# Expert products in plain float32 on two column halves, and expert weights stored in load order

## The chip, the cores and the metric

The kernel runs on one core of a Trainium2 chip. The metric is the device time of one execution, in microseconds (us), as the median of several runs. The engines are named as in the profile: PE is TensorE's matrix multiply, PEld its weight load, DVE is VectorE, ACT is ScalarE, POOL is GpSimd, and SP is the engine whose queue starts nearly all loads.

## What is computed

512 tokens of width 1024 pass through two blocks. The first has two layers, each with a gated recurrence, three kinds of attention and a feed-forward part. The second has two attentions, a cross attention to a memory, and at its end a mixture of 32 experts. The change touches the experts alone. The reference for one expert and its tokens is

```python
def expert_block(args):
    xb, e = args
    hb = jax.nn.silu(xb @ w_gate[e]) * (xb @ w_up[e])
    return hb @ w_down[e]
```

Every token goes to two experts of one group, and the two results are added with weights `row_w` to the residual; a last norm follows. `w_gate` and `w_up` are 1024 x 512 per expert and `w_down` is 512 x 1024, all float32, so that one expert has 3 x 2 MB (6.29 MB) of weights and all 32 have 201 MB. All of it is read in each run, since each expert gets tokens.

## The kernel before

The scheduler of the language sets the order of the instructions on each engine; buffers come from pools whose sizes stand in `CAPS` (SBUF) and `PSUM_BUFS` (PSUM). A tile is written again only when all that read it are done, and this is how loads are held back: a load on SP waits until its buffer is free.

The experts stand in `moe`. Routing makes lists of up to 64 places (`CAP`) per expert. Then a loop over the 32 experts runs. `gather` (L1485, an indirect DMA that POOL issues) brings the expert's token rows from `x_d` into one of two buffers `xg`. `front` transposes them on PE (L1493, eight transposes into the PSUM tile `PU`), multiplies by the norm's gain on DVE into `ex`, and runs the gate and the up product. `back` transposes the 64 x 512 hidden rows (L1520, four transposes), runs the down product, copies the result out on ACT (L1532) and scatters the rows to `y_d` with another indirect DMA from POOL (L1533). `back` of an expert comes after `front` of the next.

Every product is made of numbers split in two: `split` writes the high part of a tile in the type float32r on ACT (L258) and the remainder on DVE (L259), and `mm3` (L282 to L284) adds three products, high by high, low of the one by high of the other and the reverse. The token side is stationary, 128 x 64 (64 token places), and the weights are the moving side, 512 columns a matmul. Per expert these are 8 row blocks x 2 products x 3 plus 4 row blocks x 2 halves x 3, or 72 matmuls.

`weights` (L1475) takes a buffer `ew` of 128 x 1024 (512 KB), loads it and splits it into `ewh` and `ewl`. There are 34 buffers `ew`. A tile of the gate or up weights is two row blocks of 128 x 512, so that each partition receives two runs of 2 KB; a tile of the down weights is one row block of 128 x 1024, one run of 4 KB per partition, and 512 KB in one piece in memory. The first 34 loads are started early, in groups, each gated on an event further ahead in the program (`gate`, a copy of one column on POOL): ten, then up to 16, 24 and 32, and the last two when the lists are there.

After the loop come, in the program's text, the loads of the residual by tokens (`xt`, L1557), a diagonal matrix of the tokens' weights built by eight POOL instructions (`dg`, L1560), an identity (`idn`, L1563), a conditional block for experts with more than 64 tokens (L1576, not taken here), and the sum of both experts of each token on PE (L1597, L1606) with the last norm. All engines meet at the end of the conditional block.

Of the kernel before, what the change touches and what calls it, by code (L numbers as in the profile page):

```python
# [20 lines left out]
            hh=22, hl=22, gt=10, sq=2, fw=2, fwh=2, fwl=2, yh=8, yl=8, mgh=8, mgl=8, MKH=4, MKL=4, yt=4, xt=4, ew=34, ew1=16, ew2=24, ew3=32, xgs=2, ewh=3, ewl=3, exh=2, exl=2, esg=2, ex=2, ehh=2, ehl=2, ey=3, fs=4, fo=4)  # L21
# steps of a layer of the first block, see Net.layer1
# [9 lines left out]
# ---------------------------------------------------------------- host layout  # L32
# Constants that depend on shapes alone, and inputs rearranged (no arithmetic).
# [5 lines left out]
def _constants():  # L39
# [56 lines left out]
    # what the last phase needs comes first  # L96
# [10 lines left out]
def _masks():  # L107
    """[128, 3, 128]: causal mask, strictly earlier rows, identity; and the forget rows' selectors"""
    p = np.arange(128)
    m = np.zeros((128, 10, 128), np.float32)  # L110
    m[:, 0] = np.where(p[None, :] > p[:, None], NEG, 0.0)
    m[:, 1] = p[:, None] < p[None, :]
    for h in range(8):
        m[h, 2 + h] = 1.0
        m[32 + h, 2 + h] = 1.0
    return m
# [41 lines left out]
def _chunks(w, starts, size=128):  # L158
    """[K, N] -> per chunk [128, K/128 * size]: the blocks of a column chunk, K blocks in order."""
# [4 lines left out]
def _flat(w, width=1024):  # L164
    """[n, 128, W] -> tiles of `width` columns of the row of blocks."""
    a = w.transpose(1, 0, 2).reshape(128, -1)
    return np.ascontiguousarray(a.reshape(128, -1, width).transpose(1, 0, 2))


def _layout(inp):  # L170
# [46 lines left out]
    o["eg"] = x["w_exp_gate_2"][0]  # L217
    o["eu"] = x["w_exp_up_2"][0]
    o["ed"] = x["w_exp_down_2"][0]
# [7 lines left out]
# ---------------------------------------------------------------- the kernel  # L227


class Net:  # L230
# [3 lines left out]
    # ---- small helpers  # L234
# [4 lines left out]
    def column(self, n):  # L239
        """a few columns of their own, for the whole program"""  # L240
# [3 lines left out]
    def after(self, t, gate):  # L244
        """t's first write comes after `gate` is there."""
# [8 lines left out]
    def split(self, hi, lo, src, scale=None):  # L254
        """hi + lo = src (* scale per partition), both float32r."""
# [8 lines left out]
    def wload(self, ap, width, lane=""):  # L264
        """weights in two parts; lane f: buffers of their own, for products that fill other phases' gaps"""
# [12 lines left out]
    def mm3(self, ps, wst, wmv, first, last):  # L278
        """ps += (h + l of stationary)(h + l of moving), three passes."""
# [30 lines left out]
    def wstream(self, ap, lane=""):  # L310
        """blocks [128, 128] of tiles ap[n][128, 1024] in order."""
# [7 lines left out]
    def chunk(self, stream, xs, n=512, out=None):  # L319
        """one column chunk of 128 outputs: W^T x, x a list of (hi, lo)."""  # L320
# [5 lines left out]
    # ---- norm: x * gain in two parts, and 1/rms apart  # L326
# [26 lines left out]
    def sums(self, ps, sq, ones, nb, w=1, rows=slice(0, 128)):  # L353
        """column sums of sq [.., nb * 128] by token: ps[:, (b w)] = sq_b^T ones"""
# [3 lines left out]
    def rows(self, r):  # L358
        """columns r[t, i] as rows [i, t] of a scratch in memory"""
# [11 lines left out]
    def spread_pe(self, ps, r, nb, rows=128, stride=1, at=0):  # L371
        """ps[:rows, (b t)] = r[t, b], the same in every partition"""
# [6 lines left out]
    def spread(self, out, d, nb, at=0, stride=1):  # L379
        """out[p, (b t)] = row b of d, the same in every partition"""  # L380
# [4 lines left out]
    def rsqrt(self, out, ms, scale, eps):  # L385
        """out = (ms * scale + eps) ** -0.5 on a few columns: first guess from the bits, three Newton steps."""
# [16 lines left out]
    def tokens(self, ap, ntile, kper, n, xs, rtok, nb, evac, lane=""):  # L403
        """token-major projection: out[b] [128 tokens, n], W [128, kper, n] tiles."""
# [12 lines left out]
    def half_silu(self, out, ps, rstd):  # L417
        """out = silu(ps * rstd) as (tanh(z / 2) + 1) * z / 2"""
# [19 lines left out]
    def head_sums(self, ps):  # L438
        """mean squares of raw heads by token: sums [128, (4 blocks, 2 heads)]"""
# [6 lines left out]
    def nsa_q(self, ps, gain, cos, sin, rtok):  # L446
        """raw roped q times gain as two stacks; per token and head rstd / 8."""
# [8 lines left out]
    def head_rsqrt(self, r, ms, rtok, scale, eps):  # L456
        """rtok * (rtok^2 * ms * scale + eps) ** -0.5 for [128, (4 blocks, 2 heads)]"""
# [30 lines left out]
    def q_stack(self, x, n=512):  # L488
        """heads of rows 0-63 and 64-127 -> two [hi; lo] stacks."""
# [10 lines left out]
    def k_stack(self, x, n=512, into=None):  # L500
        """per head [hi; hi] and [lo; lo]."""
# [16 lines left out]
    # ---- softmax rows  # L518
# [16 lines left out]
    def softmax_rows(self, Ps, scores, scale=None, gate=None):  # L535
        """of the four query blocks: exp(scale * (S - max)) * gate / row sum"""
# [20 lines left out]
    def softmax(self, P, S, n, scale=None):  # L557
        """exp(scale * (S - max)), its row sum's reciprocal."""
# [11 lines left out]
    def transposed(self, Ps, causal=True, two=True):  # L570
        """P of the four query blocks -> per key block ((hi, lo) or the whole, first query column)."""
# [28 lines left out]
    def values(self, n, name, two):  # L600
        """two: per head of 64 its two parts side by side"""
# [11 lines left out]
    def pv(self, out, v, p, first, last):  # L613
        """two parts: rows 0-63 high part of v times p, rows 64-127 low part of v times the high part of p"""
# [12 lines left out]
    def out_heads(self, O, row0, hi, lo):  # L627
        """O psum [64, 512] -> rows row0.. of the chunk's hi / lo."""
# [10 lines left out]
    # ---- block 1  # L639
# [37 lines left out]
    def compress(self, l, n):  # L677
        """the compressed keys [hi; hi], [lo; lo] of [128, (g 32)], and values per head."""
# [3 lines left out]
        for i, s in enumerate("kv"):  # L682
# [10 lines left out]
            # the 32nd block does not exist: its column is never used  # L693
# [73 lines left out]
    def cmp_probs(self, l, n, g):  # L767
# [4 lines left out]
        for qb in range(4):  # L772
# [18 lines left out]
            if qb == 0:  # L791
                # queries before the first whole block see none
# [6 lines left out]
    def nsa_head(self, l, n, h, hi, lo):  # L799
        """one query head: the three branches, gated, summed in one bank."""  # L800
# [16 lines left out]
    def hgrn_proj(self, l, xs, rstd):  # L817
        """log forget gates, keys and queries of the two pairs of heads."""
# [27 lines left out]
    def hgrn_levels(self, l, r):  # L846
        """A[s, t] = sum_d q_t k_s exp(b_t - b_s), s <= t, built over halved spans, two heads at a time.
# [850 lines left out]
```

## Time and profile before

| what | value |
| --- | --- |
| three runs | 2646.52, 2654.74, 2651.53 us; median 2651.53 us |
| span of the profiled execution | 2651.4 us |
| PE busy | 2582.3 us, 97% |
| DVE busy | 1816.4 us, 69% |
| ACT busy | 1334.6 us, 50% |
| POOL busy | 134.4 us, 5% |
| bytes read from memory | 370.61 MB, of which 201 MB are expert weights |

The profiled execution's own time is its span; it lies 0.1 us under the median of the runs. A PE row's busy time runs from a matmul's start to its modelled end, and successive matmuls overlap, so that the time one costs in a row of equal ones is the distance from start to start, not the duration. A plain float32 matmul of 512 columns leaves two records in the trace (for example, the eight of L1300 leave 16).

### The profile page before, as it was taken

How to read it: one execution, taken by the hardware profiler on the slowest of the kernel's cores; microseconds unless marked ns; L12 is line 12 of the kernel's file. 1: busy time of each engine (PE TensorE's matmuls, PEld its weight loads, DVE VectorE, ACT ScalarE, POOL GpSimd, SP SyncE). 2: the span in 40 equal slices, each digit the busy share in tenths (PEclk: the TensorE clock that was granted, in tenths of full speed). 3: DMA queues.
4: the chain of work that ended last, by engine and by line, in shares of the span. 5: the costliest groups of instructions: out<-in, count | busy, mean ns of one | idle time of the engine just before them, and what ended most of it. 6: DMA issues, size and time to landing. Idle time of an engine off the chain costs nothing. (4 is left out here: it accounts for less than half of the span.)

```text
span 2651.4 us, 33625 instructions
## 1 busy us (share of the span) xinstructions
PE 2582.3 (97%) x12098; PEld 1862.6 (70%) x12099; DVE 1816.4 (69%) x3496; ACT 1334.6 (50%) x2026; POOL 134.4 (5%) x199
## 2 busy tenths in 40 slices
PE   8999999999999999999999999999997999999997
PEld 6876557888888875678888877777874555555553
DVE  6778875444346888864443378677665989888986
ACT  6544553222235445442222256554443777877784
POOL 0000000000000000000000000000011110111102
PEclk9999999999999999999999999999997999999998
DMA  5132002222231231012222231222246999999996
GB/s 199 42 106 78 9 17 90 93 95 96 96 126 58 65 118 34 1 64 95 93 92 96 95 115 56 84 92 83 92 175 237 329 342 344 338 348 350 338 344 244
DMA packets 144316, 382.32 MB, mean 144 GB/s; under 512 B 15744, under 2 KB 16144, under 8 KB 143504
## 3 DMA queue, kind: packets, MB, share of 16 engines
q1 hardware_dynamic: 138160, 369.62, 41.0%
q0 software_dynamic: 5120, 8.40, 1.0%
q10 hardware_dynamic: 864, 2.10, 0.3%
q8 instruction: 96, 1.57, 0.2%
q14 instruction: 76, 0.62, 0.1%
HBM read 370.61 MB, written 12.59 MB: 145 GB/s over the span
## 5 line engine op out<-in xcount | busy, mean ns | idle before, releaser
L258 ACT ACTIVATE wh<-w 128x1024 fp32r<-128x1024 f32 (+1 forms) x264 | 276.5, 1048 | 642.8 <-PE mm L283 352.0
L282 PE MATMUL mm<-xh,wh 128*128 128x512 f32 x1232 | 494.7, 402 | 9.9 <-ACT wh L258 9.9
L283 PE MATMUL mm<-xl,wh 128*128 128x512 f32 x1232 | 493.7, 401 | 0.0
L284 PE MATMUL mm<-xh,wl 128*128 128x512 f32 x1232 | 491.3, 399 | 0.7 <-DVE wl L259 0.7
L259 DVE TENSOR_TENSOR ewl<-ew,ewh 128x1024 fp32r<-128x1024 f32 x384 | 450.8, 1221 | 50.5 <-ACT ewh L258 48.1
L259 DVE TENSOR_TENSOR wl<-w,wh 128x1024 fp32r<-128x1024 f32 (+1 forms) x264 | 319.6, 1211 | 172.8 <-ACT wh L258 171.6
L258 ACT ACTIVATE ewh<-ew 128x1024 fp32r<-128x1024 f32 x384 | 377.8, 1047 | 14.3 <-PE mm L284 5.1
L282 PEld LDWEIGHTS mm<-xh,wh 128*128 128x128 f32 x1232 | 232.8, 189 | 66.6 <-ACT wh L258 10.0
L283 PEld LDWEIGHTS mm<-xl,wh 128*128 128x128 f32 x1232 | 232.6, 189 | 55.5 <-issue 2.9
L284 PEld LDWEIGHTS mm<-xh,wl 128*128 128x128 f32 x1232 | 232.7, 189 | 54.0 <-DVE wl L259 1.5
L252 DVE TENSOR_TENSOR tmp<-mm,xrstd 128x512 f32<-128x512 f32 x104 | 71.6, 690 | 250.6 <-PE mm L284 244.1
L283 PE MATMUL mm<-hl,wh 128*128 128x512 f32 x352 | 138.6, 394 | 0.0
L282 PE MATMUL mm<-hh,wh 128*128 128x512 f32 x352 | 138.3, 393 | 0.0
L284 PE MATMUL mm<-hh,wl 128*128 128x512 f32 x352 | 138.2, 393 | 0.0
L549 ACT ACTIVATE P<-S,st,const 128x128 f32<-128x128 f32 (+3 forms) x128 | 78.5, 616 | 52.7 <-DVE st L252 43.0
L282 PE MATMUL mm<-ewh,exh 128*64 128x512 f32 x256 | 102.0, 398 | 1.8 <-ACT exh L258 1.8
L282 PE MATMUL S<-ewh,ehh 128*64 128x512 f32 x256 | 102.4, 400 | 1.0 <-ACT ehh L258 1.0
L283 PE MATMUL mm<-ewl,exh 128*64 128x512 f32 x256 | 102.5, 400 | 0.0
L284 PE MATMUL mm<-ewh,exl 128*64 128x512 f32 x256 | 101.8, 398 | 0.4 <-DVE exl L259 0.4
L283 PE MATMUL fmm<-ewl,exh 128*64 128x512 f32 x256 | 101.6, 397 | 0.0
L282 PE MATMUL fmm<-ewh,exh 128*64 128x512 f32 x256 | 100.6, 393 | 0.5 <-ACT ewh L258 0.5
L284 PE MATMUL fmm<-ewh,exl 128*64 128x512 f32 x256 | 100.6, 393 | 0.0
(514 smaller groups left out, 4779.7 us busy)
## 6 DMA issues: line engine op xcount, KB each, us to landing
ew<-in_eg_dram SPq DMA_DIRECT2D x128, 512.0 KB
ew<-in_eu_dram SPq DMA_DIRECT2D x128, 512.0 KB
ew<-in_ed_dram SPq DMA_DIRECT2D x128, 512.0 KB
w<-in_fi_dram SPq DMA_DIRECT2D x88, 512.0 KB
w<-in_w_dram SPq DMA_DIRECT2D x48, 512.0 KB
w<-in_fo_dram SPq DMA_DIRECT2D x44, 512.0 KB
w<-in_c_dram SPq DMA_DIRECT2D x16, 512.0 KB
tmp<-tmp SPq DMA_DIRECT2D x80, 64.0 KB
```

What stands on the lines that cost most here:

```text
L252: (eng or self.nc.vector).tensor_tensor(out, a, b, op=op)
L258: nc.scalar.activation(hi, src, AF.Copy)
L259: nc.vector.tensor_tensor(lo, src, hi.bitcast(F32), op=OP.subtract)
L282: nc.tensor.matmul(ps, ah, bh, start=first, stop=False)
L283: nc.tensor.matmul(ps, ah, bl, start=False, stop=False)
L284: nc.tensor.matmul(ps, al, bh, start=False, stop=last)
L549: nc.scalar.activation(Ps[q0 + i], S[:, :n], AF.Exp, bias=b, scale=1.0 if scale is None else scale[q0 + i], accum_out=st[:, 1, i:i + 1])
```

## The change

The expert matmuls use plain float32 tiles: nothing is split, and one `matmul` stands where `mm3` stood. The gate product writes PSUM partitions 0 to 63 and the up product partitions 64 to 127 of one PSUM tile, that is, the 64 stationary columns of the one lie in the left half of the array and those of the other in the right half, and the two take turns. The down product does the same with its two halves of 512 columns. Each expert now has 24 such matmuls. The factor 1/rms of a token is applied to the gathered rows on ACT (L1487) and no longer behind the product. The hidden rows are copied out of PSUM once (L1513). The gate and up loads alternate on SP.

The host lays the three weight arrays out as [expert, 4, 128, 1024], so that each load of 512 KB is one piece in memory with one run of 4 KB per partition. There are 40 buffers `ew`, and 8 of them (before: 2) wait for the lists. Comments and docstrings are gone too; lines that held them are empty or removed, and this moves no instruction.

```diff
-            hh=22, ..., ew=34, ew1=16, ew2=24, ew3=32, xgs=2, ewh=3, ewl=3, exh=2, exl=2, esg=2, ex=2, ehh=2, ehl=2, ey=3, fs=4, fo=4)
+            hh=22, ..., ew=40, ew1=16, ew2=24, ew3=32, xgs=2, esg=2, eh=2, ex=2, ehT=2, ey=3, fs=4, fo=4)
...
-    o["eg"] = x["w_exp_gate_2"][0]
-    o["eu"] = x["w_exp_up_2"][0]
-    o["ed"] = x["w_exp_down_2"][0]
+    for n, w in (("eg", "gate"), ("eu", "up"), ("ed", "down")):
+        e = x[f"w_exp_{w}_2"][0]
+        o[n] = np.ascontiguousarray(e.reshape(NE, -1, 128, e.shape[2]).transpose(0, 2, 1, 3).reshape(NE, 128, 4, 1024).transpose(0, 2, 1, 3))
...
         def weights(ap):
             w = self.tile([128, 1024], F32, name="ew")
...
-            nc.sync.dma_start(w.rearrange("p (a b) -> p a b", b=ap.shape[-1]), ap)
-            wh = self.tile([128, 1024], F32R, name="ewh")
-            wl = self.tile([128, 1024], F32R, name="ewl")
-            if self.nw <= CAPS["ewh"]:
-                self.gate(wh, rt)
-                self.gate(wl, ready)
-            self.split(wh, wl, w)
-            return wh, wl
+            nc.sync.dma_start(w, ap)
+            return w
...
+        one, two_ = slice(0, CAP), slice(CAP, 2 * CAP)
+
         def front(xg, li_e, wg, wu, pool="mm"):
+            nc.scalar.activation(xg[:CAP], xg[:CAP], AF.Copy, scale=li_e[2])
             pt = self.mmT(self.ptn)
...
-            self.split(xh.rearrange(f3), xl.rearrange(f3), x.rearrange(f3))
-            pss = []
-            for w3 in (wg, wu):
-                ps = self.mmT(pool)[:CAP]
-                for t in range(4):
-                    wh, wl = weights(w3[:, 2 * t:2 * t + 2, :])
-                    for kk in range(2):
-                        k = 2 * t + kk
-                        ws = slice(kk * 512, kk * 512 + 512)
-                        self.mm3(ps, (xh[:, k, :], xl[:, k, :]), (wh[:, ws], wl[:, ws]), k == 0, k == 7)
-                pss.append(ps)
-            sg = self.tile([CAP, 512], F32, name="esg")
-            nc.scalar.activation(sg, pss[0], AF.Silu, scale=li_e[2])
-            nc.vector.scalar_tensor_tensor(sg, pss[1], li_e[2], sg, op0=OP.mult, op1=OP.mult)
-            return sg
+            ps = self.mmT(pool)
+            for t in range(4):
+                ws = [weights(w3[t]) for w3 in (wg, wu)]
+                for kk in range(2):
+                    k = 2 * t + kk
+                    for r, w in zip((one, two_), ws):
+                        nc.tensor.matmul(ps[r], x[:, k, :], w[:, kk * 512:kk * 512 + 512], start=k == 0, stop=k == 7)
+            sg = self.tile([128, 512], F32, name="esg")
+            nc.scalar.activation(sg[two_], ps[one], AF.Silu)
+            h = self.tile([CAP, 512], F32, name="eh")
+            self.tt(h, ps[two_], sg[two_], OP.mult)
+            return h
...
-            py = [self.mmT("S")[:CAP] for _ in range(2)]
+            hT = self.tile([128, 4, CAP], F32, name="ehT")
+            nc.vector.tensor_copy(hT.rearrange(f3), pt[:, :256])
+            py = self.mmT("S")
             for k in range(4):
-                wh, wl = weights(wd[:, k:k + 1, :])
-                for half in range(2):
-                    ws = slice(half * 512, half * 512 + 512)
-                    self.mm3(py[half], (hh[:, k, :], hl[:, k, :]), (wh[:, ws], wl[:, ws]), k == 0, k == 3)
+                w = weights(wd[k])
+                for i, r in enumerate((one, two_)):
+                    nc.tensor.matmul(py[r], hT[:, k, :], w[:, i * 512:i * 512 + 512], start=k == 0, stop=k == 3)
```

The order on PE around the border of two experts in the middle of the loop, before. `mm` and `S` are PSUM tiles of the gate and of the down product, `PU` takes transposes, `exh` and `ehh` are the high parts of the tokens and of the hidden rows:

```order
L282 MATMUL mm<-ewh,exh 64x512
L283 MATMUL mm<-ewl,exh 64x512
L284 MATMUL mm<-ewh,exl 64x512
L1520 MATMUL PU<-const,esg 128x64 x3
L1493 MATMUL PU<-const,xg_15883 128x64 x8
L282 MATMUL S<-ewh,ehh 64x512
L283 MATMUL S<-ewl,ehh 64x512
```

The same engine and place now. `mm` and `fmm` hold gate and up side by side, `eh` are the hidden rows:

```order
L1499 MATMUL mm<-ew,ex 64x512 x16
L1518 MATMUL S<-ew,ehT 64x512 x2
L1511 MATMUL PU<-const,eh 128x64 x4
L1490 MATMUL PU<-const,xg_15881 128x64 x7
L1518 MATMUL S<-ew,ehT 64x512 x2
L1490 MATMUL PU<-const,xg_15881 128x64
L1518 MATMUL S<-ew,ehT 64x512 x4
L1499 MATMUL fmm<-ew,ex 64x512 x16
```

The triples became single matmuls that read the loaded tile `ew` itself, and the last pair of a down product moved behind the next expert's sixteen gate and up matmuls.

The order on POOL at the end of the loop, before (the last scatters, then what the end of the kernel needs; `TENSOR_LOAD` reads the number that the conditional block tests):

```order
L1533 DMA y_d<-ey,const 1024x1024 x3
L1560 TENSOR_SCALAR ew<-const 128x128 x8
L1533 DMA y_d<-ey,const 1024x1024
L1575 TENSOR_LOAD cmaxi
L249 COPY idn<-ey 64x1
L1563 COPY idn<-const 128x128
L1533 DMA y_d<-ey,const 1024x1024
L1576 COMPARE_AND_BRANCH
```

And now:

```order
L1522 DMA y_d<-ey,const 1024x1024 x5
L249 COPY idn<-ey 64x1
L1552 COPY idn<-const 128x128
L1522 DMA y_d<-ey,const 1024x1024
L1549 TENSOR_SCALAR ew<-const 128x128 x8
L1564 TENSOR_LOAD cmaxi
L1565 COMPARE_AND_BRANCH
```

The eight instructions for the diagonal matrix `dg`, which stood ahead of the last two scatters, now stand behind the last one and ahead of the branch.

## Rows read from the trace of the kernel before

**Rows 1.** Page, the span in 40 equal slices, two of its rows:

```profile
DMA  5132002222231231012222231222246999999996
GB/s 199 42 106 78 9 17 90 93 95 96 96 126 58 65 118 34 1 64 95 93 92 96 95 115 56 84 92 83 92 175 237 329 342 344 338 348 350 338 344 244
```

**Rows 2.** Windows: stretch, its us, then PE, PEld, DVE, ACT, POOL, clock, DMA, GB/s:

```profile
2060.00:2600.00 540.00, 538.52 (x2513) 311.40 (x2512) 485.18 (x480) 427.86 (x510) 57.90 (x60) 1.00 0.98 343
```

**Rows 3.** Groups of PE in 2060 to 2600, by form: busy us, mean ns:

```profile
L282 PE MATMUL S<-ewh,ehh 128*64 128x512 f32 x240 | 96.0, 400 | 0.0
...
L1493 PE MATMUL PU<-const,xg 64*128 64x64 f32 x239 | 19.8, 223 | 0.0
L1520 PE MATMUL PU<-const,esg 64*128 64x64 f32 x117 | 19.4, 246 | 0.0
```

**Rows 4.** Line L1533, 2060 to 2600: count, ns min/median/max, first and last start:

```profile
L1533 POOL DMA_INDIRECT y_d<-ey,const x30: 897/924/1524, 2073.1 to 2596.1; - x30
```

**Rows 5.** Waits of SP in 2060 to 2600: waited for, us, times, longest:

```profile
SPq L1475 <- DVE ewl L259: 359.4, 274, 5.1
```

**Rows 6.** The gathers' and scatters' DMA queue in 2060 to 2600: packets, MB, share of 16 engines:

```profile
q0 software_dynamic: 4560, 7.65, 4.5%
```

**Rows 7.** Three float32 matmuls of 36 stationary columns: timeline, then their line:

```profile
1996.04 2.77 PE L1300 MATMUL tok<-h,const 128*36 128x512 f32 x6
...
L1300 PE MATMUL tok<-h,const x16: 592/592/620, 1996.0 to 2013.7; 128*36 128x512 f32 x16
```

**Rows 8.** Timeline of L377, 64 stationary columns: two halves in turn, then one alone:

```profile
215.73 1.76 PE L377 MATMUL X<-tmp,const 128*64 128x512 f32 x4
...
216.42 0.19 PEld L377 LDWEIGHTS X<-tmp,const 128*64 128x64 f32 x2 [0.52 <-DVE tmp L376]
...
274.02 1.07 PE L377 MATMUL X<-tmp,const 128*64 128x512 f32 x2
```

**Rows 9.** Windows as in Rows 2, where many loads stand in the queue:

```profile
1956.00:1974.00 18.00, 13.31 (x62) 10.74 (x60) 11.71 (x27) 5.37 (x11) 5.11 (x19) 0.88 1.04 387
1994.00:1997.00 3.00, 3.00 (x12) 1.57 (x12) 2.18 (x4) 1.08 (x2) 0.00 (x0) 1.00 1.02 418
2027.00:2031.00 4.00, 1.99 (x24) 1.91 (x20) 2.31 (x8) 0.00 (x0) 0.55 (x2) 0.50 1.03 420
```

**Rows 10.** Timeline of SP: start, us, the loads that filled these stretches, and the later ones:

```profile
1955.57 9.32 SPq L1475 DMA_DIRECT2D ew<-in_eg_dram  x4
...
1990.34 1.76 SPq L1475 DMA_DIRECT2D ew<-in_ed_dram  x4
...
2035.71 3.66 SPq L1475 DMA_DIRECT2D ew<-in_eg_dram  x3
```

**Rows 11.** Timeline of PE where the experts begin:

```profile
2038.66 0.66 PE L282 MATMUL mm<-ewh,exh 128*64 128x512 f32 x1 [0.69 <-ACT exh L258]
```

**Rows 12.** Timelines of PE, POOL and SP at the end of the kernel:

```profile
2619.37 0.40 PE L284 MATMUL S<-ewh,ehl 128*64 128x512 f32 x1
...
2620.97 0.92 POOL L1533 DMA_INDIRECT y_d<-ey,const  x1 [0.49 <-ACTq L1576]
...
2626.14 1.99 SPq L1604 DMA_DIRECT2D yt<-y_d  x4
```

**Rows 13.** Line L1560, all eight, then the three from 2606.8 on:

```profile
L1560 POOL TENSOR_SCALAR ew<-const x8: 592/1838/2535, 2597.0 to 2608.0; 128x128 f32<-128x128 f32 x8
...
L1560 POOL TENSOR_SCALAR ew<-const x3: 592/595/1324, 2605.5 to 2607.4; 128x128 f32<-128x128 f32 x3
```

**Rows 14.** Windows as in Rows 2, with PE partly idle:

```profile
1010.50:1017.40 6.90, 5.05 (x24) 2.68 (x22) 6.78 (x33) 4.23 (x12) 0.00 (x0) 1.00 0.00 0
829.60:833.00 3.40, 2.17 (x17) 1.70 (x15) 2.12 (x3) 2.77 (x3) 0.00 (x0) 1.00 0.41 126
833.10:839.80 6.70, 6.70 (x27) 6.12 (x27) 4.41 (x8) 2.59 (x4) 0.00 (x0) 0.50 0.02 6
2017.50:2044.70 27.20, 12.11 (x76) 8.76 (x77) 17.17 (x51) 6.03 (x9) 9.25 (x28) 0.50 0.77 269
```

More of the change, by code (lines that the diff above doesn't have):

```diff
@@ L20 @@
             P=2, P2=2, pth=3, ptl=3, st=8, stc=2, r4=2, rsx=3, rsy=3, rst=3, hr=2, xtok=2, mh=8, ml=8,
-            hh=22, hl=22, gt=10, sq=2, fw=2, fwh=2, fwl=2, yh=8, yl=8, mgh=8, mgl=8, MKH=4, MKL=4, yt=4, xt=4, ew=34, ew1=16, ew2=24, ew3=32, xgs=2, ewh=3, ewl=3, exh=2, exl=2, esg=2, ex=2, ehh=2, ehl=2, ey=3, fs=4, fo=4)
+            hh=22, hl=22, gt=10, sq=2, fw=2, fwh=2, fwl=2, yh=8, yl=8, mgh=8, mgl=8, MKH=4, MKL=4, yt=4, xt=4, ew=40, ew1=16, ew2=24, ew3=32, xgs=2, esg=2, eh=2, ex=2, ehT=2, ey=3, fs=4, fo=4)
 ORDER = "P0 L0 A0 V0 O0 O1 W0 K0 Q0 Q1 C0 H0 H1 H2 H3 K1 Q2 Q3 C1 H4 H5 H6 H7 R0 R1"
@@ L1493, in front, with back @@
                 nc.tensor.transpose(pt[:, k * 64:k * 64 + 64], xg[:CAP, k * 128:k * 128 + 128], self.c("ident")[:CAP, :CAP])
[L1494 to L1496 removed]
             x = self.tile([128, 8, CAP], F32, name="ex")
             self.tt(x, pt.rearrange("p (k n) -> p k n", k=8), self.p("g_ffn")[:, :, None].to_broadcast([128, 8, CAP]), OP.mult)
[L1499 to L1515 removed]
+            ps = self.mmT(pool)
[10 more added lines that the diff above has]
+            return h
+        def back(h, li_e, wd):
             f3 = "p a b -> p (a b)"
@@ L1519, in back @@
             for k in range(4):
-                nc.tensor.transpose(pt[:, k * 64:k * 64 + 64], sg[:, k * 128:k * 128 + 128], self.c("ident")[:CAP, :CAP])
-            hh = self.tile([128, 4, CAP], F32R, name="ehh")
-            hl = self.tile([128, 4, CAP], F32R, name="ehl")
-            self.split(hh.rearrange(f3), hl.rearrange(f3), pt[:, :256])
-            py = [self.mmT("S")[:CAP] for _ in range(2)]
+                nc.tensor.transpose(pt[:, k * 64:k * 64 + 64], h[:, k * 128:k * 128 + 128], self.c("ident")[:CAP, :CAP])
+            hT = self.tile([128, 4, CAP], F32, name="ehT")
+            nc.vector.tensor_copy(hT.rearrange(f3), pt[:, :256])
+            py = self.mmT("S")
             for k in range(4):
-                wh, wl = weights(wd[:, k:k + 1, :])
-                for half in range(2):
-                    ws = slice(half * 512, half * 512 + 512)
-                    self.mm3(py[half], (hh[:, k, :], hl[:, k, :]), (wh[:, ws], wl[:, ws]), k == 0, k == 3)
+                w = weights(wd[k])
+                for i, r in enumerate((one, two_)):
+                    nc.tensor.matmul(py[r], hT[:, k, :], w[:, i * 512:i * 512 + 512], start=k == 0, stop=k == 3)
             y = self.tile([CAP, D], F32, name="ey")
-            for half in range(2):
-                nc.scalar.activation(y[:, half * 512:half * 512 + 512], py[half], AF.Copy)
+            for i, r in enumerate((one, two_)):
+                nc.scalar.activation(y[:, i * 512:i * 512 + 512], py[r], AF.Copy)
             nc.gpsimd.indirect_dma_start(
@@ L1538, in wviews @@
         def wviews(e):
-            return [self.a[n][e].rearrange("(k p) f -> p k f", p=128) for n in ("eg", "eu", "ed")]
+            return [self.a[n][e] for n in ("eg", "eu", "ed")]
         lists = [[li[:CAP, 0, e:e + 1], li[:CAP, 1, e:e + 1], rtp[:CAP, e:e + 1]] for e in range(NE)]
@@ L1587, in moe @@
                         gather(xgs[0], lists)
-                        w = [v.rearrange("a k p f -> p (a k) f") for v in
-                             [self.a[n][bass.ds(e, 1)].rearrange("a (k p) f -> a k p f", p=128) for n in ("eg", "eu", "ed")]]
+                        w = [self.a[n][bass.ds(e, 1)].rearrange("a k p f -> (a k) p f") for n in ("eg", "eu", "ed")]
                         back(front(xgs[0], lists, w[0], w[1]), lists, w[2])
```

4 lines of the change are left out of this document (removed).

## The prediction

> **What bounds the kernel now.** I read the page's 40 slices first. In the last nine the DMA engines are busy nine tenths or more, at some 340 GB/s [rows 1]; that is the stage of the experts, and two suspects show: PE and the loads. The windows then say that from 2060 to 2600 us PE is busy 538.5 of 540 us at a granted clock of 1.00 (2.4 GHz), with a DMA share of 0.98 [rows 2]. A DMA share does not tell who waits for whom. SP's waits do: for 359.4 us it stood before the next load because the remainder split `ewl` on DVE had not yet released a buffer [rows 5]. So the loads are held back by their readers, the readers keep pace with PE, and PE never waits: **PE bounds the stage**. Its pace is read from the scatters, one per expert: (2596.1 − 2073.1)/29 = 18.03 us [rows 4]. The transposes of an expert take (19.8 + 19.4)/30 = 1.3 us [rows 3], which leaves 16.7 us for 72 matmuls, 0.232 us each.
>
> **PE's work per expert.** 72 split matmuls become 24 plain ones of 512 columns. The price of a plain one is in the trace of another stage: six records of L1300 take 2.77 us, the last one 0.592, so records start (2.77 − 0.592)/5 = 0.436 us apart, and two of them make a matmul of 0.87 us [rows 7]. If the two column halves exclude each other, an expert costs 24 × 0.87 + 1.3 = 22.2 us; if they run fully at once, 12 × 0.87 + 1.3 = 11.8 us. Which it is hangs on one place of the trace. L377 runs two plain float32 matmuls of 64 stationary columns on two halves. The second half's weights waited for DVE and were in at 216.42 + 0.19; the pair ended at 215.73 + 1.76 = 217.49, 1.07 us after 216.42. A lone one of the same line takes 1.07 us as well [rows 8]. Had the second half waited for the first, whose last record cannot have ended before about 216.2 + 0.59 = 216.8, it would have ended near 217.9. So the halves overlapped, though for some 0.4 us of a single pair only. I take 0.9 to 0.95 us for a pair and 12.1 to 12.7 us for an expert; both ends, 11.8 and 22.2, stay for the rivals. The pair at which nothing is gained is (18.03 − 1.3)/12 = 1.39 us.
>
> **The loads become the bound.** With PE at about 12.5 us, an expert's twelve loads decide. Before, they ran at 343 GB/s at a share of 0.98, or 350 if always busy: 512 KB in 1.50 us. That was with two thirds of the bytes in runs of 2 KB. Where many loads stand in the queue, the 2 KB runs of `eg` moved at 387 GB/s, the 4 KB runs of `ed` at 418 and 420, with PE busy or half idle [rows 9]; [rows 10] has the loads that filled the first two stretches. In the changed kernel all three arrays have the form of `ed`, and the queue is deep, since PE is quicker than the loads. At 418 GB/s a load takes 1.25 us. These rows last only 3 to 4 us, so I take 2% off and use 1.28 us; 1.25 and 1.50 us bound the range. The gathers and scatters take 4.5% of the engines, 0.045 × 540/30 = 0.81 us per expert [rows 6]. Period: 12 × 1.28 + 0.81 = 16.2 us. So of PE's gain of about 5.5 us per expert some 3.7 us are lost to the loads.
>
> The Trainium skill, "DMA: Bandwidth & Descriptors" (Bandwidth), speaks against more than about 358 GB/s from memory when both cores of a pair stream, and lets a lone core go higher; the rows with 418 and 420 agree with the lone core. By the lower figure, as an estimate, a load would take 1.46 us and the kernel about 2612 us.
>
> **Start and end of the stage.** Groups of early loads are gated as before: 32 of 384 loads are started ahead, and the next begin on SP at 2035.7 [rows 10], so 352 loads run from about 2036.5: 352 × 1.28 = 450.6 us. The gathers and scatters of 29.3 experts add 23.8. The last load lands at 2036.5 + 450.6 + 23.8 = 2510.9. PE's first expert matmul stays at about 2038.7 [rows 11], with 32 to 40 tiles in hand, and at 1.05 us per tile against 1.28 it catches up after some 150 tiles; from there it follows each load. Its cold start, clock 0.50 until 2044.7 [rows 14], is therefore hidden; without that lead it would cost some 5 us. After the last load one pair is left, 0.9 us: 2511.8.
>
> Before, the kernel ended 2651.4 − 2619.8 = 31.6 us after its last expert matmul (2619.37 + 0.40 [rows 12]). This tail stays with one addition. The eight instructions for `dg` on POOL ran before the last scatters; now they stand between the last scatter and the branch at which all engines meet, and the loads of `yt` stand behind that on SP. One takes 0.592 us when DVE is quiet, up to 2.5 when it is not [rows 13]: 8 × 0.592 = 4.7 us. The scatter's issue ended at 2621.9 and `yt` began at 2626.1 [rows 12], so POOL or the scatter's landing already took 4.2 us there. If `dg` runs beside the landing it costs about 0.5, if the landing comes first, all 4.7; I take 4. The loads of `xt` now queue behind the last expert's, 2.6 MB at 418 GB/s or 6.3 us; the branch and `yt` come later than that, which hides them. Uncovered they would cost up to 6.3.
>
> Sum: 2511.8 + 31.6 + 4 = **2547 us**, against the profiled execution's own 2651.4 (the median of the runs is 2651.53; I correct nothing for 0.1 us). The bounds: 1.25 us per load and no delay by `dg` give 2533; 1.50 us give 2036.5 + 528 + 23.8 + 36.5 = 2624.
>
> **Costed at nothing:** DVE's and ACT's splits (DVE 485 us and ACT 428 us busy of 540 [rows 2], most of it splits) stood beside PE, and nobody waits for them afterwards. The new scaling of the gathered rows on ACT is some 1 us between gather and transposes; the gather for an expert is started when the buffer of the one before is free, a period of 16 us ahead, and covers it. If the gather came late it would be 1 us per expert, 30 us in all. The 40 instead of 34 `ew` buffers add lead, not rate.
>
> **Rivals.** *Halves exclude each other (slower).* Against it stands the pair of rows 8, for it that this is one pair, overlapped briefly. 32 × 22.2 = 710 us from 2038.7, and 36 of tail: 2785 us. It decides against the change from 1.39 us per pair. *Half overlap:* two of four records at once, 3 × 0.436 = 1.31 us a pair, 17.0 us per expert, PE bound: 2038.7 + 32 × 17.0 + 36 = 2619, or a little less where transposes hide. *The loads stay near 350 GB/s* though their form is `ed`'s, because gathers and the other stream disturb them: 2624. *The clock falls while PE waits for loads.* PE's busy share would be 12.5/16.2 = 77%. With 5.05 busy of 6.90 us (73%) the clock stayed at 1.00; after 2.17 of 3.40 (64%) it was 0.50, and with 12.11 of 27.2 as well [rows 14]. At 0.50 an expert would cost twice 12.5, 25 us, so PE would no longer wait, and a PE that is always busy has 1.00 in rows 2: it would swing, and while it is slow the loads run on into 40 buffers, 51 us of lead. So this costs time only if the slow stretches are long: half of the experts at 0.50 would give (12.5 + 25)/2 = 18.75 us if the lead covers the loads throughout, 2675, slower than before; one expert in ten is hidden by the lead, and what lies between gives 2550 to 2640.
>
> The Trainium skill, "TensorE: Matmul & The Clock Gate" (HAM oscillation — how this bites in real kernels), has a kernel whose matmuls were shorter than the wait for the next load and which fell to the low clock at every step. That is the last rival; rows 14 show both outcomes here.
>
> *The change doesn't do what it says* (the matmuls are still issued so that a half waits for the other's bank or weights): this is the first rival by another road, same price.
>
> **How the numbers follow.** Forecast, loads bound at 1.25 to 1.38 us each: 0.67, its own range 2525 to 2585 us. Halves exclude, 0.08. Half overlap, 0.07. Loads near 350 GB/s, 0.08. Clock falls, 0.06, of which 0.01 slower than before and 0.01 the same. Something that eats the whole gain, such as late gathers on top of slower loads, 0.04, of which 0.03 within the bound. About ±0.3% is what a measurement of this kernel can tell from no change. Faster by more 0.87, within 0.04, slower 0.09. The range runs from 2525 (420 GB/s throughout, a tail that shrinks a little) to 2622, just short of the case of 350 GB/s; left out are the slower cases, no change, and little below.
>
> **What would show it.** Right: in the experts' stage PE has gaps that end with a DMA of `ew`; 405 to 420 GB/s; scatters 15.8 to 16.3 us apart; pairs 0.87 to 0.95 us apart in a row of sixteen; clock 1.00; SP waits for PE and hardly before the end for lack of buffers; `dg` between the last scatter and `yt`, which starts some 10 us after the last expert matmul. Wrong: pairs at 1.31 us or more (overlap), 350 GB/s with loads queued (memory), a clock of 0.50 in the stage, or gaps of PE that end with `xg`.

## The result and the profile after

The changed kernel takes 2688.93 us (median of four runs, 2683.16 to 2694.41), the kernel before 2649.03 us beside it (2646.11 to 2654.74): a ratio of 1.0142, interval 1.0119 to 1.0165. So it is 1.4% slower, where 3.9% faster was forecast, and outside the stated range. The profiled execution has a span of 2688.3 us and took 2689.91.

| what | before | after |
| --- | --- | --- |
| span of the profiled execution | 2651.4 us | 2688.3 us |
| PE busy | 2582.3 us, 97% | 2501.1 us, 93% |
| DVE busy | 1816.4 us, 69% | 1356.3 us, 50% |
| ACT busy | 1334.6 us, 50% | 969.8 us, 36% |
| one expert, scatter to scatter | 18.03 us | 19.16 us |

Neither PE nor the loads bound the stage of the experts now. Its windows (stretch, its us, then PE, PEld, DVE, ACT and POOL busy, clock, DMA share, GB/s), to be laid beside [rows 2]:

```profile
2060.00:2600.00 540.00, 437.10 (x1692) 130.61 (x1689) 51.10 (x85) 81.08 (x112) 51.66 (x56) 0.97 0.87 315
```

PE is idle for 103 us of 540, and the DMA engines for 13%, at 315 instead of 343 GB/s. When both suspects have holes, something makes each wait for the other. The scatters give the period, (2584.2 − 2067.0)/27 = 19.16 us, where [rows 4] had 18.03 (columns: count, ns least, median and most, first and last start):

```profile
L1522 POOL DMA_INDIRECT y_d<-ey,const x28: 922/927/945, 2067.0 to 2584.2; - x28
```

SP's waits name the cause. In [rows 5] there was one kind that counted, the DVE split that reads the weight buffer itself. Now (waited for, us in total, times, longest):

```profile
SPq L1475 <- DVE eh L252: 122.7, 28, 11.0
SPq L1475 <- PE fmm L1499: 87.4, 10, 10.3
SPq L1475 <- PE S L1518: 77.8, 23, 5.3
SPq L1475 <- PE mm L1499: 45.6, 7, 9.6
```

The first row is the strange one. No instruction on DVE reads a weight buffer any more, and still a load waits 28 times, once per expert, for the DVE product that writes the hidden rows `eh`. The order of SP has this wait in every expert from the ninth on (`DMAHW` is the queue's own count of landed loads, `DVE_49` and `PE_49` are waits for those engines):

```
576 L1475 DMA ew_17751<-in_ed_dram 128x1024 [waits DMAHW6_49]
577 L1475 DMA ew_17755<-in_ed_dram 128x1024 [waits DMAHW7_49]
578 L1475 DMA ew_17759<-in_ed_dram 128x1024 [waits DMAHW0_49,PE_49]
579 L1475 DMA ew_17763<-in_ed_dram 128x1024 [waits DMAHW1_49,DVE_49,PE_49]
580 L1475 DMA ew_17789<-in_eg_dram 128x1024 [waits DMAHW2_49]
581 L1475 DMA ew_17791<-in_eu_dram 128x1024 [waits DMAHW3_49]
582 L1475 DMA ew_17797<-in_eg_dram 128x1024 [waits DMAHW4_49,PE_49]
```

The addresses in the built program say why. The allocator does not give a pool a fixed block: it lays each tile wherever memory is free at that point of its planned schedule. Of the 324 expert loads that follow the first 60, 78 go to a place that a small tile, mostly of the same or a neighbouring expert, used last: `eh` 26, `ehT` 23, `ex` 23, `esg` 6. In the kernel before it is 24 of 324. Such a load waits until the small tile of the expert now at work is done with, and since SP's queue is in order, all later loads wait behind it. The other rows are the same thing: a load in the place of an `ex` waits for the gate and up matmuls that read it (`fmm` and `mm`, 133.0 us in 17 waits together, more than the first row), one in the place of an `ehT` for the down product (`S`). Laid beside the trace, load by load, the addresses account for nearly all of it: of SP's stalls over 1 us from 2060 to 2600 us, 360 us stand before a load in the place of a small tile (`ex` 143, `eh` 119, `ehT` 78, `esg` 20) and 14 us before one in the place of another load.

One turn of this in the trace: DVE and PE, then SP (start, us, engine, line, operation; in brackets the idle time before):

```profile
2319.33 1.93 PE L1499 MATMUL mm<-ew,ex 128*64 128x512 f32 x6 [0.20 <-DMA ew<-in_eu_dram]
...
2321.92 0.69 DVE L252 TENSOR_TENSOR eh<-mm,esg 64x512 f32<-64x512 f32 x1 [17.94 <-ACT esg L1501]
...
2322.67 0.46 PE L1511 MATMUL PU<-const,eh 64*128 64x64 f32 x4 [0.55 <-DVE eh L252]
...
2327.81 1.71 PE L1518 MATMUL S<-ew,ehT 128*64 128x512 f32 x4 [1.61 <-DMA ew<-in_ed_dram]
```

```profile
2310.24 13.24 SPq L1475 DMA_DIRECT2D ew<-in_ed_dram  x4
...
2321.30 2.19 SPq L1475 DMA_DIRECT2D ew<-in_ed_dram  x2
2323.54 0.42 SPq L1475 DMA_DIRECT2D ew<-in_eg_dram  x1
2324.01 0.42 SPq L1475 DMA_DIRECT2D ew<-in_eu_dram  x1
2329.55 0.33 SPq L1475 DMA_DIRECT2D ew<-in_eg_dram  x1
```

SP's first row spans all four `ed` loads with the waits between them, the second shows the last two alone. The third load goes out at 2321.30, when the last gate and up matmul has ended (2319.33 + 1.93 = 2321.26): it lies where `ex` was. The hidden rows are written at 2321.92 and transposed from 2322.67 to 2323.13. Only then, at 2323.16, does the fourth `ed` load start, and behind it the next `eg`. The fourth load's matmuls start at 2327.81, after a gap of 1.61 us. The load of 2329.55 is held a second time. So in this turn the place of `ex` holds SP longest, and the place of `eh` adds 1.5 us to it; in turns without a hold by `ex`, `eh` alone holds it for some 10 us. In the meantime the queue has run dry (windows of the same kernel):

```profile
2310.00:2320.00 10.00, 9.44 (x28) 2.31 (x27) 0.00 (x0) 1.15 (x1) 0.00 (x0) 0.95 1.00 383
2320.00:2323.00 3.00, 2.45 (x13) 0.80 (x11) 0.69 (x1) 0.59 (x1) 0.00 (x0) 1.00 0.41 89
2323.00:2329.00 6.00, 4.04 (x23) 1.16 (x20) 1.12 (x2) 0.00 (x0) 0.94 (x1) 0.93 0.84 305
```

While the loads issued so far move, both are busy; then the queue has hardly anything left (89 GB/s in the three microseconds around the restart), and after the restart PE waits for the first loads to land (4.04 of 6 us busy). By about 2120 us PE had used up its lead: of 89 loads issued it was done with 80. Between 2150 and 2500 us two to ten loads, five in the median, are issued and not yet used up, of forty buffers (in `ring40` below it is eight to seventeen, ten in the median). Most loads are used 3 to 12 us after their issue, which is hardly more than they take to land.

Where the lead was still there, the trace shows the pace of PE that was forecast:

```profile
2050.47 7.09 PE L1499 MATMUL fmm<-ew,ex 128*64 128x512 f32 x32 [0.78 <-DVE ex L252]
...
2058.51 3.65 PE L1518 MATMUL S<-ew,ehT 128*64 128x512 f32 x16
```

32 records are eight pairs in 7.09 us, 16 are four in 3.65: 0.89 and 0.91 us a pair with the end of the last one, against 0.87 for one matmul alone in [rows 7].

### The profile page after: what moved, and what is told of

Its sections match the earlier page's. It is cut to its first block, busy times and chain, and to the rows that moved or that the text cites. A ratio compares the mean times of both kernels' runs of the same rounds, so it can differ in the third digit from the quotient of the medians.

```text
span 2688.3 us, 30462 instructions
## 1 busy us (share of the span) xinstructions
PE 2501.1 (93%) x11330; PEld 1677.3 (62%) x11331; DVE 1356.3 (50%) x3080; ACT 969.8 (36%) x1610; POOL 123.6 (5%) x199
## 5 line engine op out<-in xcount | busy, mean ns | idle before, releaser
L1499 PE MATMUL mm<-ew,ex 128*64 128x512 f32 x512 | 170.2, 651 | 28.0 <-DMA ew<-in_eu_dram 16.9
L1499 PE MATMUL fmm<-ew,ex 128*64 128x512 f32 x512 | 163.6, 618 | 35.1 <-DMA ew<-in_eu_dram 22.0
L1518 PE MATMUL S<-ew,ehT 128*64 128x512 f32 x512 | 148.6, 639 | 37.6 <-DMA ew<-in_ed_dram 36.7
L1499 PEld LDWEIGHTS mm<-ew,ex 128*64 128x64 f32 x512 | 45.2, 145 | 152.9 <-issue 63.6
L1499 PEld LDWEIGHTS fmm<-ew,ex 128*64 128x64 f32 x512 | 42.8, 138 | 154.0 <-DMA ew<-in_eu_dram 67.6
L252 DVE TENSOR_TENSOR eh<-fmm,esg 64x512 f32<-64x512 f32 x16 | 11.1, 693 | 217.1 <-ACT esg L1501 217.0
L252 DVE TENSOR_TENSOR eh<-mm,esg 64x512 f32<-64x512 f32 x16 | 11.1, 693 | 212.4 <-ACT esg L1501 212.3
L1521 ACT ACTIVATE ey<-S 64x512 f32<-64x512 f32 x64 | 37.8, 590 | 173.3 <-PE S L1518 160.6
L1518 PEld LDWEIGHTS S<-ew,ehT 128*64 128x64 f32 x512 | 32.6, 139 | 93.7 <-DMA ew<-in_ed_dram 64.0
```

Source lines behind the costliest of these rows:

```text
L252: (eng or self.nc.vector).tensor_tensor(out, a, b, op=op)
L1499: nc.tensor.matmul(ps[r], x[:, k, :], w[:, kk * 512:kk * 512 + 512], start=k == 0, stop=k == 7)
L1518: nc.tensor.matmul(py[r], hT[:, k, :], w[:, i * 512:i * 512 + 512], start=k == 0, stop=k == 3)
L1521: nc.scalar.activation(y[:, i * 512:i * 512 + 512], py[r], AF.Copy)
```

## The experiments

Theory A: shared places hold up SP. Theory B: memory gives no more in this mixture. Theory C: the clock and the staggered pairs set the time. Medians below are of the kernel's own runs, ratios are to the kernel before, run beside it.

**Forty fixed buffers, `ring40`.** The loads go round through buffers that belong to them alone:

```diff
...
-            w = self.tile([128, 1024], F32, name="ew")
-            if self.nw < CAPS["ew"]:
+            if self.nw >= CAPS["ewr"]:
+                w = ring[self.nw % CAPS["ewr"]]
+                self.nw += 1
+                nc.sync.dma_start(w, ap)
+                return w
+            w = self.tile([128, 1024], F32, name="ewr")
+            ring.append(w)
+            if self.nw < CAPS["ewr"]:
```

> The changed kernel, with one edit: the expert weights go round through 40 fixed buffers, so that load n waits only for the readers of load n-40, and no small tile (tokens, hidden rows) lies in a weight buffer's place. Theory A (in the changed kernel SP's queue is held up once or twice per expert by loads whose place was last used by a small tile of the current expert, so that PE has no loads in hand): SP's waits for DVE `eh` are gone, loads land every 1.25 to 1.30 us at 405 to 420 GB/s, 16 us per expert, 2530 to 2570 us. Theory B (memory gives no more than about 320 GB/s with two streams in turn and the gathers): SP's waits go, but the rate stays, 2660 to 2700 us. Theory C (the falls of the clock to 0.50, and pairs that wait for two loads each, set the time): mean clock stays at 0.93 to 0.97 in the stage and the time at 2640 to 2700 us.

2567.42 us, ratio 0.9687 (0.967 to 0.9704): 121 us less than the changed kernel, and 3.1% faster than the kernel before. SP's waits and the stage:

```profile
SPq L1476 <- DMA ewr<-in_eg_dram: 116.1, 103, 2.4
SPq L1476 <- DMA ewr<-in_eu_dram: 104.5, 104, 2.2
SPq L1476 <- DMA ewr<-in_ed_dram: 98.1, 104, 1.9
```

```profile
2100.00:2500.00 400.00, 354.92 (x1492) 116.01 (x1494) 46.33 (x77) 71.62 (x99) 45.80 (x49) 0.99 1.03 391
```

The waits for `eh` are gone. SP waits almost only for the queue to take more, the DMA engines are always busy (1.03) and move 391 GB/s. B falls. The loads are the bound, as forecast for the change itself. PE works off the same pairs in the same order, so the staggered pairs of C do not set the time either; the clock of C is left, since it rose too, from 0.97 to 0.99.

**One half of the array, `ring36_onehalf`.** Every product in the left column half, each in a PSUM tile of its own:

```diff
-            ps = self.mmT(pool)
+            ps = [self.mmT(pool)[:CAP] for _ in range(2)]
...
-                    for r, w in zip((one, two_), ws):
+                    for r, w in zip((0, 1), ws):
```

> Fixed buffers (36, since the extra tiles leave less room), and gate and up, and the two halves of the down product, all on the left column half (each in a PSUM tile of its own): nothing can overlap. If two column halves run at once in the changed kernel, PE becomes the bound at 24 x 0.87 + 1.3 = 22.2 us per expert, 2770 to 2800 us with PE without gaps. If they do not overlap anyway, the time is that of the 40 fixed buffers.

2773.39 us, ratio 1.0467 (1.0449 to 1.0484). PE is the bound, without gaps, and the down product that took 3.65 us takes twice as long:

```profile
2100.00:2500.00 400.00, 395.08 (x1091) 133.05 (x1090) 29.01 (x54) 50.88 (x72) 33.71 (x36) 1.00 0.91 300
...
2307.41 7.08 PE L1526 MATMUL S<-ewr,ehT 128*64 128x512 f32 x16 [0.27 <-DVE ehT L1521]
```

So the two column halves do run at once; that is worth 206 us here (with 36 buffers instead of 40), and it is what lets the loads become the bound.

**The layout alone, `before_layout`.** The kernel before, with the weights in contiguous blocks and the products still split:

```diff
-            nc.sync.dma_start(w.rearrange("p (a b) -> p a b", b=ap.shape[-1]), ap)
+            nc.sync.dma_start(w, ap)
```

> The kernel before with the weights in contiguous blocks of 512 KB alone; products split in three as before. If PE bounds the experts of the kernel before: 2640 to 2655 us, within 0.3% of it, though the loads now have the quicker form, and SP waits as long for DVE `ewl`, with a lower DMA share (below 0.9). If the loads were a part of the bound there: 2560 to 2630 us.

2649.73 us, ratio 1.0003 (0.9991 to 1.0015): no change. The DMA share falls only from 0.98 to 0.96 at the same 343 GB/s, so a share near 1 with PE as the bound said little about what the loads could do (I had expected under 0.9):

```profile
2060.00:2600.00 540.00, 538.52 (x2507) 311.23 (x2506) 483.95 (x479) 426.00 (x508) 61.89 (x62) 1.00 0.96 343
```

**The old layout, `ring40_oldlayout`.** The forty fixed buffers with the weights as in the kernel before, two runs of 2 KB for gate and up (the edit above the other way round).

> The 40 fixed buffers with the weights as the kernel before has them in memory: gate and up loads of two runs of 2 KB per partition. With loads as the bound at 17.0 us per expert, two thirds of the bytes at 387 instead of 410 GB/s cost 0.05 x 8 x 1.28 to 0.09 x 8 x 1.28 or 0.6 to 0.9 us per expert, 2585 to 2600 us. If the form of the loads does not matter at this depth of the queue: 2560 to 2572 us.

2582.08 us, 14.7 us over `ring40` and just under what was expected. The layout is worth 0.5 us per expert once the loads are the bound (380 against 391 GB/s from 2100 to 2500 us), and nothing as long as PE is.

**The wait put back by hand, twice.** First with a copy on POOL, `ring40_held`:

```diff
+                if held is not None:
+                    self.gate(w, held)
                 nc.sync.dma_start(w, ap)
...
-                w = weights(wd[k])
+                w = weights(wd[k], h if k == 3 else None)
```

> The 40 fixed buffers, with the wait put back by hand and no shared place: the fourth `ed` load of each expert is preceded by a one-column copy on POOL that reads that expert's hidden rows `eh`, so this load, and all behind it on SP, start only after them. Theory A: the lead is gone again, 2640 to 2710 us, SP waits for POOL 8 to 11 us per expert. Theories B and C: within 0.5% of the 40 fixed buffers without the wait.

2573.56 us, 6 us over `ring40`. This is a miss, by which B or C would have been right; I put it down to the experiment. `back` runs one expert late, so its own `eh` is a whole gate and up product old when its loads are issued; the wait that SP shows in the changed kernel is for the `eh` of the expert that `front` has just finished. For that the transposes have to stand at the end of `front`, which is the control `ring40_T`:

```diff
+            pt = self.mmT(self.ptn)
+            for k in range(4):
+                nc.tensor.transpose(pt[:, k * 64:k * 64 + 64], h[:, k * 128:k * 128 + 128], ...)
...
-            return h
+            return h, hT
```

> Control for the next kernel: the 40 fixed buffers, and the four transposes of an expert's hidden rows written at the end of `front` instead of the start of `back`; no wait is added. Every theory: within 0.5% of the 40 fixed buffers (2567 us), 2555 to 2580 us.

2571.42 us, 4 us over `ring40`. Then the one place is shared, in `ring40_T_eh`:

```diff
-            h = self.tile([CAP, 512], F32, name="eh")
+            at = self.nw + 3
+            h = ring[at % CAPS["ewr"]][:CAP, :512] if CAPS["ewr"] <= at < 380 else self.tile([CAP, 512], F32, name="eh")
```

> As the control, but the hidden rows `eh` of an expert are written into the fixed buffer that the last `ed` load of the expert before is to fill, so that this load, once per expert, waits for the product on DVE and the four transposes: the same wait that SP shows in the changed kernel, and nothing else. (The copy on POOL of the earlier kernel named the rows of the expert before, which are there a whole gate and up product earlier, and cost next to nothing.) Theory A: per expert the loads start again only when the hidden rows are transposed: some 4.5 us until the first lands, eight of gate and up at 1.3, a last pair 0.9 and 2 us to the next hidden rows, 17.8 to 19 us, so 2630 to 2690 us, clock falls are back and PE has under 12 us of loads in hand. If one wait per expert is not the cause: within 0.5% of the control.

2659.02 us, ratio 1.0035 (1.0021 to 1.0049). One shared place per expert costs 88 us against `ring40_T`, and the kernel is back just behind the one before. The picture of the changed kernel is back with it, in windows and SP's waits:

```profile
2100.00:2500.00 400.00, 325.62 (x1244) 98.39 (x1240) 37.33 (x62) 60.97 (x84) 38.61 (x41) 0.98 0.88 325
```

```profile
SPq L1476 <- DVE ewr L252: 219.7, 21, 11.8
```

SP is held 21 times, once per expert, for 10.5 us on average (the tile is called `ewr` here, since `eh` lies in it). The falls of the clock that were expected with it did not come: 0.98.

**The rest.** The changed kernel has two more kinds of shared places. In `ring40_T_eh_ex` the tokens `ex` lie in the place of the third `ed` load, in `ring40_T_eh_ehT` the transposed rows `ehT` in that of an `eg` load:

```diff
-            x = self.tile([128, 8, CAP], F32, name="ex")
+            at = self.nw + 10
+            x = ring[at % CAPS["ewr"]][:, :8 * CAP].rearrange("p (a b) -> p a b", a=8) if 64 <= at < 380 else ...
```

> As the kernel with `eh` in the place of the last `ed` load (2659 us), and the tokens `ex` of the same expert in the place of the third, which so waits for the last gate and up matmul: two loads behind the hold instead of one, as in the changed kernel (23 of its loads from the 60th on lie where an `ex` was). If these shared places make up the rest of the 30 us up to the changed kernel's 2689: one more load of 1.3 us is late per expert, 20 to 40 us more, 2680 to 2700 us. If the rest has another cause (the clock, the way the pairs stand): within 0.3% of 2659.

> As the kernel with `eh` in the place of the last `ed` load (2659 us), and the transposed hidden rows `ehT` in the place of the third load of the expert after next (an `eg` load), which so waits for the end of a down product. In the changed kernel such a load stands behind the hold already and waits up to 5 us more; here the scheduler also moves these loads two or three places back on SP. If this second hold makes up the rest: 2670 to 2700 us. If the move back lets other loads pass, or it is no cost: 2640 to 2665 us.

2676.50 us (ratio 1.0098, 1.0072 to 1.0124) and 2675.82 us (1.0095, 1.0074 to 1.0116): 17 us each. For `ex` that is a little less than the 20 to 40 expected, for `ehT` it is inside the range. Added to 2659 they make 2693, against 2689 of the changed kernel; this is a sum, and no run has all three kinds in fixed buffers, or `ex` without `eh`. These two kernels have the same time, and their clocks differ by much:

```profile
2100.00:2500.00 400.00, 328.77 (x1220) 94.84 (x1218) 36.33 (x61) 60.28 (x83) 39.22 (x42) 0.99 0.88 321
```

```profile
2100.00:2500.00 400.00, 304.05 (x1221) 100.39 (x1222) 36.19 (x61) 58.52 (x83) 38.94 (x42) 0.86 0.89 325
```

The first is `ex` with 0.99, the second `ehT` with 0.86. If the clock set the time, as C has it, the second would have to be the slower, so C falls for these two kernels. Why their clocks differ is not shown; the second has one gap of PE of some 4 us per expert, the first none over 2 us.

**What the gathers cost.** `ring40` has the loads as the bound, but at 17.08 us per expert ((2498.2 − 2207.9)/17 of its scatters), not 16.2. Slices of 1 us from 2300 to 2340, in the view of the transfers:

```profile
GB/s 418 410 401 414 410 410 414 377 389 418 397 336 295 291 332 410 414 418 410 401 410 410 397 414 401 406 401 397 352 258 266 266 344 414 406 414 418 397 389 397
```

Between times 410 GB/s hold, the forecast's rate. Twice, for 4 to 5 us, it falls to 260 to 350, some 3 us after a gather (`xg`) starts on POOL, and just as a scatter (`y_d`) starts there:

```profile
2307.74 0.94 POOL L1487 DMA_INDIRECT xg<-x_d,const  x1 [13.35 <-PE PU L1498]
2310.86 0.93 POOL L1530 DMA_INDIRECT y_d<-ey,const  x1 [2.17 <-ACT ey L1529]
2325.22 0.94 POOL L1487 DMA_INDIRECT xg<-x_d,const  x1 [13.43 <-PE PU L1498]
2328.39 0.92 POOL L1530 DMA_INDIRECT y_d<-ey,const  x1 [2.23 <-ACT ey L1529]
```

This row alone does not tell the gather from the scatter. Two kernels leave out 29 of the 32 gathers and keep the scatters. `ring40_nogather` also put the scaled rows into a tile of their own, in the buffers `ey`:

```diff
-            if e + 1 < NE:
+            if e < 2:
                 gather(xgs[(e + 1) % len(xgs)], lists[e + 1])
```

> The 40 fixed buffers with the gathers of 29 of the 32 experts left out (they work on the rows of the second and third gather); the scatters stay, and the scaled rows go to a tile of their own. The gathers are about half of the small queue's bytes. By the prediction's 0.81 us per expert for gathers and scatters together this saves 0.4 x 29 = 12 us, 2553 to 2558 us. If they cost what is missing between 15.4 us (twelve loads at 410 GB/s) and the 17.0 us per expert measured, or 1.6 us: 0.8 x 29 = 23 us, 2540 to 2547 us. If they cost nothing, and the loads themselves are slower than 410 GB/s: 2563 to 2570 us.

2607.67 us, useless for the question: the tile shared its buffers with the scatters' rows, PE waited 53.9 us for it from 2100 to 2500, and the loads were no longer the bound. `ring40_nogather2` leaves the gathers out and nothing else.

> The 40 fixed buffers with the gathers of 29 of the 32 experts left out, and nothing else changed (the rows of the second and third gather are scaled in place again and again; the earlier kernel of this kind put the scaled rows where the scatters' rows are, and PE waited for those). By the prediction's 0.81 us per expert for gathers and scatters together: 0.4 x 29 = 12 us less than 2567, 2552 to 2558 us. If they cost what is missing between 15.4 us (twelve loads at 410 GB/s) and 17.0 us per expert: 0.8 x 29 = 23 us less, 2540 to 2548 us. If they cost nothing, and the loads themselves are slower than 410 GB/s: 2563 to 2570 us.

2538.52 us, 28.9 us less than `ring40`, or 1.0 us per gather: more than the larger of the expected sizes, and more than the prediction gave to gather and scatter together.

```profile
2100.00:2500.00 400.00, 369.71 (x1576) 121.59 (x1572) 46.77 (x78) 74.82 (x105) 24.65 (x29) 1.00 1.02 408
```

The same slices from 2300 to 2340, and the scatters from 2200 to 2500 (columns as above):

```profile
GB/s 406 410 410 410 406 406 401 422 389 418 410 422 414 401 414 410 418 401 393 406 418 406 406 414 414 406 414 426 401 410 406 422 401 406 422 393 397 410 414 401
...
L1530 POOL DMA_INDIRECT y_d<-ey,const x19: 900/900/901, 2210.3 to 2495.6; - x19
```

Three scatters start in these 40 us, at 2305.87, 2321.49 and 2337.47, and the rate stays at 389 or more. So a scatter by itself does not lower it to a visible degree, and the falls need the gather. An expert takes (2495.6 − 2210.3)/18 = 15.85 us, 1.2 us less than in `ring40`.

**The tail, `ring40_dg`.** The diagonal matrix four experts before the end:

```diff
+            if e == NE - 4:
+                dg = self.tile([128, D], F32, name="ew")
+                for i in range(8):
+                    nc.gpsimd.tensor_scalar(dg[:, i * 128:i * 128 + 128], ...)
```

> The 40 fixed buffers, with the eight POOL instructions for `dg` written four experts ahead of the end, so that nothing stands between the last scatter and the branch. If they cost what the prediction said, 3 to 4.7 us less after the last expert matmul: the loads of `yt` start 5.5 to 7 us after it instead of some 10, 2560 to 2565 us. If the landing of the last scatter holds the branch anyway: no change in that distance.

2566.81 us, ratio 0.9682 (0.9665 to 0.9698), not to be told from `ring40` by its time. The trace tells more: the loads of `yt` start 9.7 us after the last down product (2537.94, which ends at 2528.27), with `dg` in the way 11.7 (2543.70 and 2531.98 in `ring40`). So `dg` costs 2.0 us. Of the other 9.7, 4.4 pass until the last scatter is issued (2531.75 + 0.90 on POOL), and 5.3 from there to `yt`, which fits the scatters' landing, a median of 6.4 us after their start in `ring40`.

`ring40` and `ring40_dg` beat both kernels, by 4.5% the changed one and by 3.1 to 3.2% the one before.

## Why the prediction was wrong

Most of the prices were right, and the premise that put them together was false: that loads run without a stop.

- **What bounds the kernel before**: right. With the layout alone, quicker loads changed nothing (1.0003).
- **PE's pair at 0.87 to 0.95 us**: right, 0.89 and 0.91 where PE had loads in hand; the overlap that rested on one pair of [rows 8] is shown by the kernel on one half, 2773 us where the first rival had 2785.
- **"With 32 to 40 tiles in hand ... from there it follows each load"**, and "The 40 instead of 34 `ew` buffers add lead, not rate": this is the step that failed, and with it the period of 12 × 1.28 + 0.81 = 16.2 us, which was 19.16. It took for granted that a load waits only for the readers of its own buffer, 40 loads earlier; the section on the kernel before says the same of a load on SP. In fact the place of a load may last have held a small tile of the expert now at work. PE used up its lead by about 2120 us, and from then on SP's queue was held once or twice per expert and PE waited for loads. Fixed buffers give 2567 us, inside the forecast's own range of 2525 to 2585; one shared place per expert gives 2659, two kinds 2676, and the costs of all three added 2693, where 2689 were measured. None of the rivals was this. The nearest, gaps of PE that end with `xg`, looked at the wrong transfer.
- **It could have been seen without a run.** DVE's only use of a weight buffer was the split, and the change removes it. That the order of SP in the built program of the changed kernel still has `DVE_49` in front of one `ed` load per expert, as shown above, says that this load waits for something else. I looked at the orders of PE and POOL, where instructions moved, and not at what SP's loads wait for. I also read PE's order wrongly in the section on the change: the last pair of a down product did not move behind the next expert's gate and up; the transposes of the next hidden rows moved ahead, between the first pair and the other three of the down product before.
- **A load at 1.28 us**: right between the gathers (410 GB/s in `ring40`).
- **0.81 us per expert for gathers and scatters**: mis-sized. It was taken from their share of busy time [rows 6]. A gather alone takes 1.0 us from the loads by the time saved, 1.2 by the period, since for 4 to 5 us the sum of both queues falls by up to 37%. Without gathers an expert still takes 15.85 us, 0.5 over twelve loads at 1.28. So the term should have been some 1.5 to 1.7 us. Over 29.3 experts that is 20 to 26 us more than forecast; the last expert matmul of `ring40` ended at 2531.98 instead of 2511.8.
- **The tail**: 31.6 + 4 forecast, 2688.3 − 2653.6 = 34.7 measured. `dg` itself is 2.0 us by `ring40_dg`, where I took 4 between 0.5 and 4.7, so that the sum came out better than this part of it.
- **The clock**: PE was idle nearly as often as that rival wanted (81% busy, 77% there), and the mean granted clock was 0.97 in the stage, where half of the experts at 0.50 were needed for a time like this. The two kernels with 0.86 and 0.99 and one time show that such a difference need not cost anything in a stage of this kind; for the changed kernel itself it was not tried.

The Trainium skill, "DMA: Bandwidth & Descriptors" (Bandwidth), gives a lone core about 425 GB/s on a large transfer; the 410 GB/s between the gathers are near it, and pass the 358 GB/s of a core whose pair streams too, by which the prediction estimated 2612 us.

## What to carry to other kernels

A pool's number of buffers is lead only if nothing else is laid in its memory. When a change makes the readers of a stream quicker, look in the order of the loading queue for waits on engines that do not read the stream, and give the stream fixed buffers that go round. In a queue in order all later loads stand behind one such wait: here one per expert, 10.5 us long, cost 88 us over the 32 experts.

## What was not expected of the hardware

- An indirect gather of about 32 rows of 4 KB on average (1024 places over 32 experts) takes 1.0 us from a saturated load queue, though its packets are 2 to 3% of the bytes; the total falls from 410 to between 260 and 350 GB/s for 4 to 5 us. A scatter of as many rows, without a gather beside it, left it at 389 or more.
- A DMA share of 0.98 at 343 GB/s in the kernel before left room for 380 GB/s with loads of the same form (`ring40_oldlayout`), and 0.96 at 343 in `before_layout` for 391 (`ring40`): the share did not tell what the engines could move.
- In `ring40_nogather`, where PE stood still for 2.3 us per expert, the mean granted clock was 0.80 from 2100 to 2500; in `ring40`, with shorter gaps (all but one under 1.6 us), 0.99.
